# Two attention mixers and an output projection: the exponential's bias taken in VectorE's pass over the scores, one region for transposed weights, and an output projection in one-bank halves

## The chip, the cores and the metric

One Trainium2 chip; the kernel runs on one of its cores. The metric is the device time in microseconds of one execution. The program is compiled once, in one launch, and all its work is on the chip.

## What is computed

One layer of an encoder is applied to two request groups with the same weights: the prompt (2048 rows of 1024) and the sample (512 rows of 1024). Cut to what matters:

```python
h = rmsnorm(x, g_pre) * (1 + scale) + shift          # scale, shift, gate from silu(c) @ w_ada + b_ada
qa, ka, va, ga, qb, kb, vb, gb = split(h @ w_in)     # A: 8 heads of 64; B: 4 heads of 2 x 64
# A: three dilated windows (128, 1), (512, 4), (2048, 16), mixed by their softmax denominators
ya = dilated_mixture(rope(qa), rope(ka), va) * silu(ga)
# B: dense, two softmax maps per head
p = softmax(q @ k.T / 8)
a = p[map 0] - lam * p[map 1]
yb = rmsnorm(a @ vb, g_sub) * (1 - lam_init) * silu(gb)
y = concat(ya, yb) @ w_out
x = x + gate * rmsnorm(y, g_post)
```

## The kernel before

The work is cut into eight units, taken in the order A, B, A, B, ... (`ORDER`). A unit is two heads of A or one head of B, for both request groups. Each unit runs over five superblocks of 512 rows: four of the prompt (`p`), one of the sample (`s`). An item of B is 128 rows of queries against all keys (four items a superblock); an item of A is 128 rows of one head against its windows (eight items a superblock). Numbers are held as a high and a low half of 16 bits, so a product is made of two or three matrix products.

`ItemB.front` (lines 558 to 613) makes, for each of two maps, scores in tiles of 1024 columns (`sc`, PSUM, three tiles of two banks; two tiles a map for the prompt). L584 takes the maximum of each tile on VectorE, L587 on GpSimd makes the bias of the exponential from the maxima of both tiles, L592 on ScalarE takes the exponential with that bias into an `pp` buffer (five of 4 KB) and adds up the denominators. L609 combines the two maps, L611 writes the high half (`hi`), which a DMA transposes into a tile `at`; `tail1` (L619) does the same for the low half. `tail2` (L623 to L645) multiplies the transposed weights with V: 48 matmuls at L631, then a Square and a Copy on ScalarE and three small steps on GpSimd. `tail3` scales, transposes on TensorE (L652), multiplies by the gate into `yt`, and after the fourth item `y_out` writes `y` to DRAM.

`ItemA.front` has its scores at L686 and L692; L698 and L700 on VectorE add the masks in float32 and take the maxima in one pass each, L704 on GpSimd makes the bias, L707 on ScalarE the exponential. `tail1` (L710) normalises into a high and a low half and transposes both by DMA (L725, L726); `tail2` multiplies with V after every fourth item (L742, L748).

`run_items` sets the order of an item's steps beside those of the items before it: the item's first scores; at "mid" `tail2` and `tail3` of the item two before if that is an A item, or `tail3` alone if it is a B item, then `tail1` of the item just before; the second scores; at "late" `tail2` of the item just before if that is a B item. The pool `at` has three buffers of the largest tile, 6 KB; each item of B and each head of A takes two tiles.

Beside the items, as "fill", run the projections of the next superblock (`qg_proj`) and of the next unit (`kv_proj`), in PSUM tiles `pj` of one bank, of which there is one. `interleave` emits items and fill in proportion to their costs (`mc`, `fc`). In the last unit there is no next unit, and from the third superblock on the fill is the output projection (`out_proj`) of the superblock two before, in tiles of 128 rows: `y_first` loads `y` into a `w` buffer (four of 8 KB, which also hold the projection's weights and the rows `GG`) and splits it (L872, L873); 48 matmuls at L889 fill a score tile; Square (L896), the norm's factor (L898 to L901), a product (L902) and a sum (L903) follow, and L904 stores. Eight tiles remain for the end (L1052). The program is scheduled by the framework from this order of emission; each engine and SP's DMA queue run their instructions in order.

## Time and profile before

| | us |
|---|---|
| median of 3 runs | 2272.92 |
| lowest and highest run | 2272.75, 2280.08 |
| the profiled execution, its own time | 2281.88 |
| its span, first to last instruction | 2280.1 |
| TensorE busy | 1896.0 (83%) |
| VectorE busy | 1491.4 (65%) |
| ScalarE busy | 1191.5 (52%) |
| GpSimd busy | 533.1 (23%) |
| mean granted clock of TensorE | 0.933 |

PE is TensorE's matmuls, PEld its weight loads, DVE is VectorE, ACT ScalarE, POOL GpSimd, SP the queue that issues DMAs. A wait "X <- Y" is idle time of X's engine that ended when Y's work was done. Durations come from the one profiled execution, and sums are made against its time.

### The profile page before, as it was taken

What the parts mean: (1) busy time and instruction counts of PE and PEld (TensorE: products, weight loads), DVE (VectorE), ACT (ScalarE), POOL (GpSimd) and SP (SyncE); (2) the same over time, 40 slices, a digit from 0 to 9 for tenths busy, and PEclk for the clock granted to TensorE, in tenths of its full rate; (3) what the DMA queues carried; (4) which work ended last, traced back from release to release, by engine and by line L of the source; (5) the groups of instructions that cost most, each with busy time, mean ns of one, the idle gap of its engine ahead of it and who ended that gap; (6) DMA issues with size and microseconds to landing.
All of it is one profiled execution on the core that took longest, in us unless ns stands there. A gap on an engine that the chain in (4) does not pass through costs nothing. (4 is left out here: it accounts for less than half of the span.)

```text
span 2280.1 us, 47414 instructions
## 1 busy us (share of the span) xinstructions
PE 1896.0 (83%) x18545; PEld 1291.5 (57%) x18545; DVE 1491.4 (65%) x3084; ACT 1191.5 (52%) x2238; POOL 533.1 (23%) x1369
## 2 busy tenths in 40 slices
PE   4878888888889888887888798887887887678988
PEld 2665665555666665565676655555666554334433
DVE  3775566788856558777664578876565578555533
ACT  3555554566655546665654466664555466434321
POOL 1222122223322222222421122323222132111200
PEclk8989999999999999998999899999999998789989
DMA  8488895666779877666778766688898586354433
GB/s 325 167 278 165 163 211 118 129 132 137 161 141 187 148 196 139 134 139 149 143 166 162 172 145 148 119 184 200 180 181 191 123 161 134 70 142 101 139 118 119
DMA packets 726833, 360.11 MB, mean 158 GB/s; under 512 B 639808, under 2 KB 686672, under 8 KB 723152
## 3 DMA queue, kind: packets, MB, share of 16 engines
q1 hardware_dynamic: 726608, 357.08, 68.4%
q8 instruction: 145, 2.38, 0.4%
q14 instruction: 80, 0.66, 0.1%
HBM read 164.79 MB, written 36.97 MB: 88 GB/s over the span
## 5 line engine op out<-in xcount | busy, mean ns | idle before, releaser
L439 PE MATMUL pj<-w,h 128*128 128x256 f16 x3840 | 480.9, 283 | 33.0 <-DVE sg L539 11.4
L439 PEld LDWEIGHTS <-h 128*128 128x128 f16 x3840 | 382.0, 102 | 110.4 <-issue 46.9
L584 DVE TENSOR_REDUCE mx<-sc 128x1 f32<-128x1024 f32 (+1 forms) x288 | 329.9, 1159 | 119.9 <-PE sc L582 119.3
L592 ACT ACTIVATE pp<-sc,nb,us 128x1024 f32<-128x1024 f32 (+1 forms) x288 | 330.4, 1150 | 135.0 <-POOL nb L587 133.4
L631 PE MATMUL pv<-V,at 128*128 128x128 f16 x3072 | 223.7, 232 | 70.6 <-DMA at<-hl 60.9
L631 PEld LDWEIGHTS <-at 128*128 128x128 f16 x3264 | 209.7, 104 | 118.4 <-DMA at<-hl 84.0
L513 PE MATMUL pj<-w,h 128*128 128x128 f16 x3840 | 246.1, 222 | 14.6 <-ACT q L519 6.6
L724 DVE SCALAR_TENSOR_TENSOR hl<-pp,Z,hl 128x640 f16<-128x640 f32 (+2 forms) x160 | 141.6, 887 | 173.9 <-DMA at<-hl 125.1
L534 PE MATMUL pj<-h,w 128*128 128x512 f16 x960 | 230.8, 395 | 22.8 <-ACT q L519 22.8
L513 PEld LDWEIGHTS <-h 128*128 128x128 f16 x3840 | 227.1, 100 | 37.9 <-issue 33.6
L722 ACT ACTIVATE hl<-pp,Z 128x640 f16<-128x640 f32 (+2 forms) x160 | 130.9, 824 | 185.7 <-DMA at<-hl 151.6
L576 PE MATMUL sc<-K,Qc 128*128 128x512 f16 x512 | 160.3, 393 | 65.2 <-ACT pp L592 64.8
L422 POOL TENSOR_TENSOR rp<-q,tab_sb 128x64 f32<-128x64 f32 x160 | 68.9, 431 | 598.3 <-ACT q L445 408.1
L611 ACT ACTIVATE hl<-pp,rz 128x1024 f16<-128x1024 f32 (+1 forms) x144 | 156.1, 1096 | 67.6 <-issue 50.9
L619 DVE SCALAR_TENSOR_TENSOR hl<-pp,rz,hl 128x1024 f16<-128x1024 f32 (+1 forms) x144 | 174.3, 1222 | 22.0 <-ACT hl L611 12.4
L707 ACT ACTIVATE pp<-pp,nb,us 128x640 f32<-128x640 f32 (+2 forms) x160 | 146.2, 914 | 74.3 <-POOL nb L704 73.3
L534 PEld LDWEIGHTS <-w 128*128 128x128 f16 x960 | 94.5, 101 | 140.3 <-issue 48.2
L609 DVE SCALAR_TENSOR_TENSOR pp<-pp,rz,pp 128x1024 f32<-128x1024 f32 (+1 forms) x144 | 170.9, 1224 | 1.8
L889 PEld LDWEIGHTS <-w 128*128 128x128 f16 x960 | 94.5, 99 | 118.0 <-issue 8.9
L587 POOL TENSOR_SCALAR nb<-mx,us 128x1 f32<-128x1 f32 x160 | 87.4, 547 | 266.1 <-DVE mx L584 245.9
L704 POOL TENSOR_SCALAR nb<-mx,us 128x1 f32<-128x1 f32 x160 | 74.3, 465 | 211.6 <-DVE mx L700 169.8
L889 PE MATMUL sc<-raw,w 128*128 128x512 f16 x480 | 112.9, 392 | 4.0 <-ACT pp L592 3.2
(198 smaller groups left out, 2752.6 us busy)
## 6 DMA issues: line engine op xcount, KB each, us to landing
h<-hp SPq DMA_DIRECT2D x124, 512.0 KB, 5.6
pp<-in_x_p_dram SPq DMA_DIRECT2D x32, 512.0 KB, 5.3
raw<-in_w_in_dram SPq DMA_DIRECT2D x8, 2048.0 KB, 8.6
h<-hs SPq DMA_DIRECT2D x32, 512.0 KB, 5.7
out_dram<-pp SPq DMA_DIRECT2D x20, 512.0 KB, 2.8
at<-hl SPq DMA_TRANSPOSE x608, 3.2
hp<-h SPq DMA_DIRECT2D x4, 2048.0 KB, 8.0
yp<-yt SPq DMA_DIRECT2D x32, 256.0 KB, 2.4
```

The lines of the kernel that those rows point to most:

```text
L439: mm(ps[:, jj, :], lhsT=hT[:, a, k, j * P:(j + 1) * P], rhs=w[:, k, b, :], start=(k == 0 and i == 0), stop=(k == KT - 1 and i == 2))
L513: mm(ps[:, jj, 0:128], lhsT=hT[:, a, k, j * P:(j + 1) * P], rhs=w[:, k, b, 0:128], start=(k == 0 and i == 0), stop=(k == KT - 1 and i == 2))
L534: mm(ps, lhsT=w[:, k, b, 128:256], rhs=hT[:, a, k, :], start=(k == 0 and i == 0), stop=(k == KT - 1 and i == 2))
L576: mm(ps[:, n * 512:(n + 1) * 512], lhsT=Qc[:, j, m, 0, :], rhs=K[:, t:t + 4, m, :], start=True, stop=False)
L584: V.reduce_max(mx[:, hf:hf + 1], ps[:, :HW], axis=AX.X)
L592: act(pt[m, hf][:, :HW], pss[hf][:, :HW], AF.Exp, scale=u["sc"], bias=nb, accum_out=Z[:, 2 * m + hf:2 * m + hf + 1])
L609: V.scalar_tensor_tensor(a, a, rz[:, 2:3], pt[0, hf][:, :HW], op0=ALU.mult, op1=ALU.add)
L611: act(hi[:, :HW], a, AF.Copy, scale=rz[:, 3:4])
L619: V.scalar_tensor_tensor(lo[:, :HW], a, sg, hi, op0=ALU.mult, op1=ALU.subtract)
L631: mm(po[:, :128], lhsT=a[:, k, :], rhs=Vv[:, k, 128 * b:128 * b + 128], start=(k == 0 and i == 0), stop=(k == NT - 1 and i == 2))
L707: act(sb[:, :NA], sb[:, :NA], AF.Exp, scale=u["sc"], bias=nb, accum_out=Z[:, 0:1])
L889: mm(ps[:, 512 * h:512 * h + 512], lhsT=a[:, k, :], rhs=b, start=(k == 0 and i == 0), stop=(k == KT - 1 and i == 2))
```

## The change

In B the pass over a score tile becomes one VectorE instruction that multiplies the scores by the negated scale, writes them back over the tile in PSUM and keeps the minimum; the pass over the second tile starts from the first's minimum, which is then the bias. In A both masked passes multiply by the negated scale and take the minimum, the second from the first's; the query's scale and the masks are adapted, and the masks are stored in 16 bits. The GpSimd instruction is gone in both, and the exponential takes scale -1. The pool `at` becomes one region of 24 KB, cut in three pairs of 4 KB tiles for B and two pairs of 6 KB tiles for A. B's V products (`tail2`) go from "late" of the next item to "mid" of the item after that, `tail3` from "mid" to "late" there. The output projection is one generator over all tiles: it starts in the second superblock of the last unit as far as `y` has been made (`y_made`), gets a budget per superblock (`OPC`), works in halves of one bank in `pj`, and takes `w` buffers for `x` and the result while items run. After the items PSUM is divided anew, with five `pj` banks.

```diff
@@ -26,9 +26,10 @@
 MCA = [1, 1]
-PPB, HLB, ATB, WPB, HB = 5, 4, 3, 4, 2
+PPB, HLB, WPB, HB = 5, 4, 4, 2
 AQ = 1
 LEAD = [0, 0, 0, 0]
+OPC = [0, 20, 24, 24, 30]
 ORDER = (0, 4, 1, 5, 2, 6, 3, 7)
@@ -45,6 +46,7 @@
     SMAX = max(SQ.values())
+    NU = len(ORDER)
     NTM = SMAX // P
@@ -54,11 +56,28 @@
     hl = ctx.enter_context(tc.tile_pool(name="hl", bufs=HLB))
-    at = ctx.enter_context(tc.tile_pool(name="at", bufs=ATB))
+    at = ctx.enter_context(tc.tile_pool(name="at", bufs=1))
     tn = ctx.enter_context(tc.tile_pool(name="tn", bufs=6))
...
     dr = ctx.enter_context(tc.tile_pool(name="dr", bufs=1, space=DRAM))
+    at_buf = at.tile([P, 12288], F16, tag="at", name="at")
+    at_n = {3: 0, 2: 0}
+    def at_pair(n, *dims):
+        i = at_n[n]
+        at_n[n] = (i + 1) % n
+        w = 12288 // n // 2
+        out = []
+        for x in range(2):
+            t = at_buf[:, (2 * i + x) * w:(2 * i + x) * w + math.prod(dims)]
+            names = "abc"[:len(dims)]
+            out.append(t.rearrange(f"p ({' '.join(names)}) -> p {' '.join(names)}",
+                                   **dict(zip(names[1:], dims[1:]))))
+        return out
     PS = {}
@@ -320,12 +339,14 @@
             V.reciprocal(rs, s[:, 2:3])
+            smul(s[:, 1:2], s[:, 1:2], 2.0 * LN2)
             m0, m9 = (0, 992) if r == "p" else (480 - 32 * (SQ[r] // P - 1), 480 + SQ[r] // 4)
-            mk = T(qp, [P, m9 - m0 + 768], F32, "mask" + r, bufs=1)
-            nc.sync.dma_start(mk[:, 0:m9 - m0], m23[:, m0:m9])
-            nc.sync.dma_start(mk[:, m9 - m0:], m1.rearrange("p a b -> p (a b)"))
-            V.tensor_scalar(mk, mk, rs, LN2, op0=ALU.mult, op1=ALU.mult)
+            mk = T(qp, [P, m9 - m0 + 768], BF16, "mask" + r, bufs=1)
+            for src, dst in ((m23[:, m0:m9], mk[:, 0:m9 - m0]), (m1.rearrange("p a b -> p (a b)"), mk[:, m9 - m0:])):
+                t = T(pp, [P, 1024], F32, "pp")[:, 0:src.shape[1]]
+                nc.sync.dma_start(t, src)
+                V.tensor_scalar(dst, t, rs, 0.5, op0=ALU.mult, op1=ALU.mult)
             u["m23"], u["m0"] = mk[:, 0:m9 - m0], m0
@@ -516,7 +537,9 @@
             q32 = T(ev, [P, 2, 2, 64], F32, "q32")
-            act(q32.rearrange("p a b d -> p a (b d)"), ps[:, :, 0:128], AF.Copy, scale=2.0 ** -19)
+            act(q32.rearrange("p a b d -> p a (b d)"), ps[:, :, 0:128], AF.Copy,
+                scale=2.0 ** -19 * (1.0 if g >= 4 else 0.5 / LN2))
             rope(q32, TAB0[r] + t0)
@@ -542,10 +565,13 @@
     yam = C([P, sum(NSB.values()), 8], F32, "yam")
+    y_made = {}
     def y_out(r, g, c, y):
...
         nc.sync.dma_start(y_dram[r][c][:, g, :], y)
+        y_made[r, c] = y_made.get((r, c), 0) + 1
@@ -566,7 +592,7 @@
             for m in range(2):
-                mx = T(tn, [P, 2], F32, "mx")
+                nb = T(tn, [P, 2], F32, "nb")
                 pss = []
@@ -581,15 +607,15 @@
                            start=False, stop=True)
-                    V.reduce_max(mx[:, hf:hf + 1], ps[:, :HW], axis=AX.X)
+                    V.tensor_scalar(ps[:, :HW], ps[:, :HW], u["nsc"], nb[:, 0:1] if hf else 3e38,
+                                    op0=ALU.mult, op1=ALU.min, accum_out=nb[:, hf:hf + 1])
                     yield 0.43 * (HW // 512)
-                nb = T(tn, [P, 1], F32, "nb")
-                nc.gpsimd.tensor_scalar(nb, mx[:, 0:1], mx[:, NH - 1:NH], u["nsc"], op0=ALU.max, op1=ALU.mult)
                 if m == 0:
...
                     pt[m, hf] = T(pp, [P, 1024], F32, "pp")
-                    act(pt[m, hf][:, :HW], pss[hf][:, :HW], AF.Exp, scale=u["sc"], bias=nb,
+                    act(pt[m, hf][:, :HW], pss[hf][:, :HW], AF.Exp, scale=-1.0, bias=nb[:, NH - 1:NH],
                         accum_out=Z[:, 2 * m + hf:2 * m + hf + 1])
@@ -601,8 +627,7 @@
             nc.gpsimd.tensor_tensor(rz[:, 3:4], rz[:, 0:1], sigc, op=ALU.mult)
-            self.ah = T(at, [P, S // P, P], F16, "at")
-            self.al = T(at, [P, S // P, P], F16, "at")
+            self.ah, self.al = at_pair(3, S // P, P)
             self.lo = []
@@ -693,18 +718,17 @@
             sb = self.sb = T(pp, [P, 1024], F32, "pp")
-            mx = T(tn, [P, 2], F32, "mx")
+            nb = T(tn, [P, 2], F32, "nb")
             mo = 480 - 32 * b + P * k0 - u["m0"]
             V.tensor_tensor_reduce(sb[:, :Cc], ps[:, o:o + Cc], u["m23"][:, mo:mo + Cc],
-                                   1.0, -3e38, ALU.add, ALU.max, mx[:, 0:1])
+                                   u["nsc"], 3e38, ALU.add, ALU.min, nb[:, 0:1])
             V.tensor_tensor_reduce(sb[:, Cc:NA], ps[:, m1],
                                    u["m1"][:, 0 if b == 0 else 2 if b == NB - 1 else 1, :],
-                                   1.0, -3e38, ALU.add, ALU.max, mx[:, 1:2])
-            nb = T(tn, [P, 1], F32, "nb")
-            nc.gpsimd.tensor_scalar(nb, mx[:, 0:1], mx[:, 1:2], u["nsc"], op0=ALU.max, op1=ALU.mult)
+                                   u["nsc"], nb[:, 0:1], ALU.add, ALU.min, nb[:, 1:2])
             yield "mid"
             self.Z = Z = T(tn, [P, 4], F32, "Z")
-            act(sb[:, :NA], sb[:, :NA], AF.Exp, scale=u["sc"], bias=nb, accum_out=Z[:, 0:1])
+            act(sb[:, :NA], sb[:, :NA], AF.Exp, scale=-1.0, bias=nb[:, 1:2], accum_out=Z[:, 0:1])
             yield "late"
@@ -713,8 +737,7 @@
             if ("ah", h) not in st:
-                st["ah", h] = T(at, [P, 4, Cc // P + 2, P], F16, "at")
-                st["al", h] = T(at, [P, 4, Cc // P + 2, P], F16, "at")
+                st["ah", h], st["al", h] = at_pair(2, 4, Cc // P + 2, P)
             smul(Z[:, 1:2], Z[:, 0:1], 2.0 ** -14)
@@ -780,16 +803,15 @@
                 if x == "mid":
+                    if p2:
+                        yield from p2.tail2()
                     if isinstance(p2, ItemA):
-                        yield from p2.tail2()
-                        yield from p2.tail3()
-                    elif p2:
                         yield from p2.tail3()
...
                 elif x == "late":
-                    if isinstance(p1, ItemB):
-                        yield from p1.tail2()
+                    if isinstance(p2, ItemB):
+                        yield from p2.tail3()
                 else:
@@ -874,33 +896,44 @@
     def out_proj(tiles):
-        nxt = y_first(*tiles[0])
-        yield 0.0
+        nxt = None
         for n, (r, c, j) in enumerate(tiles):
+            while nxt is None:
+                if y_made[r, c] == NU:
+                    nxt = y_first(r, c, j)
+                else:
+                    yield 0.65
             yh, yl = nxt
+            nxt = None
             s = YS[r, c]
-            xt = T(pp, [P, D], F32, "pp")
+            if PS["w"] == 512:
+                xt, jk = T(pp, [P, D], F32, "pp"), T(pp, [P, D], F32, "pp")
+            else:
+                t = T(wp, [P, 2, D], F32, "w")
+                xt, jk = t[:, 0, :], t[:, 1, :]
             nc.sync.dma_start(xt, xv[r][c, :, j, :])
-            ps = PT([P, PS["w"]], "sc")
+            ss = T(tn, [P, 2], F32, "ss2")
             for h in range(2):
+                ps = PT([P, 512], "pj")
                 for k in range(KT):
...
                     for i, (a, b) in enumerate(((yh, wh), (yh, wl), (yl, wh))):
-                        mm(ps[:, 512 * h:512 * h + 512], lhsT=a[:, k, :], rhs=b,
+                        mm(ps, lhsT=a[:, k, :], rhs=b,
                            start=(k == 0 and i == 0), stop=(k == KT - 1 and i == 2))
                     yield 0.65
-                    if h == 0 and k == 0 and n + 1 < len(tiles):
+                    if nxt is None and n + 1 < len(tiles) and y_made[tiles[n + 1][:2]] == NU:
                         nxt = y_first(*tiles[n + 1])
-            jk = T(pp, [P, D], F32, "pp")
-            ss = T(tn, [P, 1], F32, "ss")
-            act(jk, ps, AF.Square, accum_out=ss)
+                sq = T(hl, [P, 512], F32, "hl")
+                act(sq, ps, AF.Square, accum_out=ss[:, h:h + 1])
+                V.tensor_mul(jk[:, 512 * h:512 * h + 512], ps, GG[r][:, 512 * h:512 * h + 512])
             v = T(tn, [P, 1], F32, "rv")
-            V.tensor_scalar(v, ss, s[:, 2:3], EPS, op0=ALU.mult, op1=ALU.add)
+            V.tensor_add(v, ss[:, 0:1], ss[:, 1:2])
+            V.tensor_scalar(v, v, s[:, 2:3], EPS, op0=ALU.mult, op1=ALU.add)
             o = T(tn, [P, 1], F32, "ro")
...
             nc.gpsimd.tensor_tensor(o, o, s[:, 0:1], op=ALU.mult)
-            V.scalar_tensor_tensor(jk, ps, o, GG[r], op0=ALU.mult, op1=ALU.mult)
-            V.tensor_add(jk, jk, xt)
+            V.scalar_tensor_tensor(jk, jk, o, xt, op0=ALU.mult, op1=ALU.add)
             nc.sync.dma_start(ov[r][c, :, j, :], jk)
@@ -951,7 +984,16 @@
     NS = len(SBS)
-    NU = len(ORDER)
+    outp = out_proj([(r, c, j) for r, c in SBS for j in range(4)])
+    def upto(gen, cost):
+        while cost > 0:
+            x = next(gen, None)
+            if x is None:
+                return
+            cost -= x
+            yield x
     g0 = ORDER[0]
@@ -1020,6 +1062,8 @@
                 side = chain(load_wo(1), call(load_gg))
+            if i == 0:
+                at_n[3] = 0
             if i == 0 and g2 is not None:
@@ -1039,17 +1083,20 @@
                         fl.append(call(load_v1, r2, g2, c2))
-            if g2 is None and i >= 2:
-                tiles = [(*SBS[i - 2], j) for j in range(4)]
-                fl.append(out_proj(tiles))
-                fc += 11 * len(tiles)
+            if g2 is None and i >= 1:
+                fl.append(upto(outp, OPC[i]))
+                fc += OPC[i]
             main = run_items(items(r, g, c) + ([None, None] if n + 1 == NU and i + 1 == NS else []))
...
             interleave(main, mc, weave(chain(*fl), side), fc, LEAD[2 * (r == "p") + (g < 4)])
-    run(out_proj([(*SBS[k], j) for k in (-2, -1) for j in range(4)]))
+    for x in outp:
+        if x == 0.1:
+            break
+    psum(512, 1, 5, 2)
+    run(outp)
 # ---- launch: one core; inputs and outputs as the reference has them ----
```

## Rows read from the trace of the kernel before

**Rows 1.** The page's first part: busy time, share of the span and instructions of each engine.

```profile
PE 1896.0 (83%) x18545; PEld 1291.5 (57%) x18545; DVE 1491.4 (65%) x3084; ACT 1191.5 (52%) x2238; POOL 533.1 (23%) x1369
```

**Rows 2.** Busy time by stretches: start and end in us, length, then busy us and instructions of PE, PEld, DVE, ACT and POOL, the granted clock, the DMA engines' share and GB/s. The stretches begin with a superblock's first exponential: units A, B, A, B, A, B, A, then the last unit's five superblocks and, from 2181.00, what remains after the last item.

```profile
169.70:374.30 204.60, 172.32 (x2066) 128.25 (x2058) 121.21 (x381) 103.18 (x193) 42.26 (x125) 0.96 0.80 171
374.30:641.60 267.30, 227.62 (x2177) 155.49 (x2175) 207.68 (x302) 163.17 (x315) 80.96 (x194) 0.95 0.64 136
641.60:845.30 203.70, 174.18 (x2120) 134.36 (x2121) 120.51 (x384) 105.01 (x201) 45.51 (x130) 0.94 0.84 171
845.30:1109.10 263.80, 225.13 (x2192) 151.85 (x2190) 208.90 (x310) 163.59 (x312) 79.04 (x191) 0.95 0.65 139
1109.10:1319.50 210.40, 178.23 (x2128) 136.34 (x2126) 122.69 (x385) 106.45 (x205) 43.95 (x133) 0.93 0.78 164
1319.50:1589.30 269.80, 230.69 (x2259) 156.48 (x2260) 211.41 (x310) 164.95 (x317) 79.38 (x197) 0.97 0.71 155
1589.30:1804.60 215.30, 179.58 (x2140) 132.65 (x2133) 125.66 (x391) 111.08 (x213) 48.50 (x128) 0.94 0.84 179
1804.60:1864.00 59.40, 50.28 (x521) 32.58 (x519) 45.21 (x58) 35.59 (x63) 19.10 (x41) 0.97 0.76 163
1864.00:1914.30 50.30, 42.18 (x404) 24.94 (x404) 42.53 (x55) 35.62 (x64) 13.33 (x37) 1.00 0.67 128
1914.30:2021.10 106.80, 78.39 (x454) 40.30 (x454) 58.69 (x77) 40.89 (x70) 14.36 (x32) 0.81 0.47 111
2021.10:2119.00 97.90, 76.38 (x451) 40.40 (x449) 56.77 (x72) 40.72 (x68) 14.61 (x31) 0.84 0.42 106
2119.00:2181.00 62.00, 53.56 (x310) 26.80 (x310) 31.91 (x55) 22.08 (x52) 14.08 (x36) 0.95 0.45 135
2181.00:2280.10 99.10, 87.74 (x389) 39.17 (x389) 35.69 (x50) 17.88 (x24) 5.90 (x16) 0.93 0.33 117
```

**Rows 3.** The table of waits over the whole execution: engine, what it was about to write and the line, what ended the wait, us in total, times, longest.

```profile
ACT pp L592 <- POOL nb L587: 133.4, 86, 7.7
...
ACT pp L707 <- POOL nb L704: 73.3, 65, 5.3
PE sc L576 <- ACT pp L592: 69.9, 69, 10.1
...
PE pv L631 <- DMA at<-hl: 67.2, 38, 9.8
...
PE pv L742 <- DMA at<-hl: 44.6, 31, 3.9
```

**Rows 4.** The same table for TensorE in the last unit alone, from 1804.6 us to the end.

```profile
PE pv L631 <- DMA at<-hl: 33.1, 13, 9.8
...
PE sc L576 <- ACT pp L592: 11.1, 11, 2.4
```

**Rows 5.** Groups of instructions by line and shape: line, engine, operation, out<-in, shapes, count, busy us, mean ns of one, idle us of the engine before them and what ended it.

```profile
L584 DVE TENSOR_REDUCE mx<-sc 128x1 f32<-128x1024 f32 x256 | 308.6, 1218 | 109.0 <-PE sc L582 108.6
...
L587 POOL TENSOR_SCALAR nb<-mx,us 128x1 f32<-128x1 f32 x160 | 87.4, 547 | 266.1 <-DVE mx L584 245.9 <-DVE ag L855 8.0 <-DVE rz L601 4.9
...
L902 DVE SCALAR_TENSOR_TENSOR pp<-sc,ro,w 128x1024 f32<-128x1024 f32 x20 | 25.6, 1282 | 11.6 <-POOL ro L901 11.3
...
L873 DVE SCALAR_TENSOR_TENSOR w<-w,ys 128x1024 f16<-128x1024 f32 x20 | 25.0, 1281 | 7.7 <-ACT w L872 7.7
...
L698 DVE DVE_READ_ACCUMULATOR2_ANT mx<- 128x1 f32 x160 | 13.0, 81 | 0.0
```

**Rows 6.** VectorE's timeline around 679 us: start, duration, engine, line, operation; the second instruction reads what the first writes.

```profile
679.11 0.15 DVE L99 TENSOR_SCALAR Z<-Z 128x1 f32<-128x1 f32 x1 [0.15 <-ACT pp L707]
679.30 0.16 DVE L720 RECIPROCAL Z<-Z 128x1 f32<-128x1 f32 x1
```

**Rows 7.** The timeline from 680.9 us, in an A unit: two DMA transposes that SP issues, and between them the end of a head's V products on TensorE.

```profile
680.94 1.21 SPq L725 DMA_TRANSPOSE at<-hl  x1
...
684.29 1.06 PE L748 MATMUL pv<-at,V 128*128 128x128 f16 x16
...
685.32 1.25 SPq L726 DMA_TRANSPOSE at<-hl  x1
```

**Rows 8.** The DMA issues by line: out<-in, count, KB each, median us from issue to landing.

```profile
w<-yp SPq DMA_DIRECT2D x16, 512.0 KB, 4.3
...
maskp<-in_m_dram SPq DMA_DIRECT2D x4, 496.0 KB, 6.7
```

**Rows 9.** TensorE's timeline from 1926 us, in the last unit's third superblock; in brackets the idle time before and what ended it.

```profile
1930.47 1.04 PE L631 MATMUL pv<-V,at 128*128 128x128 f16 x8 [3.92 <-DMA at<-hl]
...
1945.43 1.04 PE L631 MATMUL pv<-V,at 128*128 128x128 f16 x8 [3.82 <-DVE ys L99]
...
1949.69 1.06 PE L889 MATMUL sc<-raw,w 128*128 128x512 f16 x2
```

**Rows 10.** SP's own waits in the last unit, from 1804 us: what it was about to issue, what ended the wait, us in total, times, longest.

```profile
SPq L871 <- PE sc L889: 76.1, 12, 15.4
```

**Rows 11.** ScalarE's timeline in the tail: the Square that follows a tile's last matmul, the split of a later tile's `y`, and the next tile's Square.

```profile
2240.41 1.02 ACT L896 ACTIVATE pp<-sc 128x1024 f32<-128x1024 f32 x1 [4.91 <-PE sc L889]
...
2244.74 1.15 ACT L872 ACTIVATE w<-w,ys 128x1024 f16<-128x1024 f32 x1 [3.21 <-DMA w<-ys]
...
2250.77 1.02 ACT L896 ACTIVATE pp<-sc 128x1024 f32<-128x1024 f32 x1 [4.88 <-PE sc L889]
```

## The prediction

> **What bounds the kernel now.** I read the busy shares first: TensorE is busy 83% of the span, VectorE 65%, ScalarE 52% [rows 1]. No engine is full, so the question is what TensorE, the fullest, waits for. The table by stretches comes next [rows 2]: A and B units alternate in its first seven rows, the last six are the last unit, superblock by superblock, with the tail. TensorE idles 130 us in the 834 us of the A units (834.0 - 704.3 busy), 117 us in the 801 us of the B units (800.9 - 683.4) and 87 us in the 475.5 us of the last unit (475.5 - 388.5). The last unit is the worst place: its third and fourth stretches take 107 and 98 us at a granted clock of 0.81 and 0.84, where the second takes 50 us at 1.00. The table of waits says what ended TensorE's idle time [rows 3]: scores wait 69.9 us for an Exp to free a score tile, B's V products 67.2 us for transposed weights, A's V products 44.6 us. Of the first two, 11.1 and 33.1 us lie in the last unit [rows 4], so 58.8 and 34.1 us are the B units'. ScalarE's Exp in turn waits 133.4 and 73.3 us for GpSimd's bias [rows 3]. So this is a loop of latencies (scores, maximum, bias, Exp, score tile free again), with TensorE its fullest member and VectorE (628.0 of 800.9 us in the B units [rows 2]) the second.
>
> **The bias.** Removed: 160 bias instructions of 547 ns on GpSimd in B [rows 5] and as many in A, and with each two hand-overs between engines ahead of Exp. Added: in B the maximum (1,218 ns on 1,024 scores) becomes a pass that also writes the negated scaled scores over the score tile. The trace of before shows no VectorE instruction that writes PSUM. Bounds for one pass: from below 1,218 ns, the reduction that reads the same tile; from above 2.50 us, the reduction and a separate pass of 1,282 ns as L902 makes from PSUM [rows 5]. It is one instruction with one stream in and one out, so L902's 1,282 is the nearest row; with the accumulator read of 81 ns [rows 5], most of which overlaps its neighbour, I take 1.34 us: +0.12 us. The Trainium skill ("VectorE: DVE Perf Modes", The TRN2 errata) gives 120 cycles plus one per element for an op out of PSUM, by estimate 1.19 us here; by that the pass would cost no more than the reduction, and nothing would be added; the page has no figure for a PSUM destination.
>
> The three B units make 192 passes of 1,024 and 24 of 512: 192 x 0.12 + 24 x 0.07 = +25 us on VectorE, then 653 us busy. A second pass now reads the first's minimum. Such a reader starts 0.04 us after its writer's end [rows 6]; with the accumulator read that is some +0.15 us, 160 times in A, 24 us on a VectorE that idles 344 of 834 us there [rows 2]: hidden. Behind it on VectorE wait the splits of the weights, whose transposes are wanted an item later. If that cover were gone (VectorE full), the price is 25 + 24 us. In exchange Exp starts earlier by the bias, 0.55 us and up (GpSimd runs it in turn behind rotary and power steps), so score tiles come free sooner: half of the 58.8 us, 29 us, goes; bounds 0 and 58.8. What is late next there is VectorE's own queue: I put 10 us back.
>
> **One region, and V products an item later.** Before, three 6 KB buffers serve tiles that come in pairs, so the second tile of a pair waits for the products of the item or head just before. In A one sees it: a `hi` transpose is issued at 680.94, the next `lo` only at 685.32, when the other head's V products end (684.29 + 1.06) [rows 7]; SP's queue is in order, so what lies behind waits too. With two pairs in A and three in B no transpose waits for the item just finished. In B the 48 V products of an item move from behind the next item's second scores to between the first and second scores of the item after that. Their Square and Copy on ScalarE and three GpSimd steps move with them; the output's transpose and the `y` store on SP move behind the second scores. That is half an item later, some 6 us of a 55 us stretch with four items, against waits of 1.4 us on average (34.1 us in 38 - 13 waits [rows 3, 4]): I let 27 of the 34.1 us go, bounds 0 and 34. TensorE also gets work at the very point where it waits for a score tile; that is part of the 29 above. In A the products keep their place, and the last transpose is still one short item ahead, so I let half of the 44.6 us go: 22 us, bounds 0 and 45. Shorter holes should return a little clock: 3 in B, 3 in A. **B: -29 + 10 - 27 - 3 = -49; A: -25.** Bounds: B 0 and -95, A +10 (dependent passes) and -55. The masks now pass through the exponentials' five buffers; a load of 6.7 us [rows 8] may hold two of them at the start and in three later units. I take +3 us, bounds 0 and +10.
>
> **Output projection.** Before, a tile holds one of three score tiles and two of five exponential buffers through its 48 matmuls and its evacuation, and each group of four tiles starts only when its stretch comes. The trace shows it: from 1,926 to 1,950 us TensorE does items alone, with holes of 3.9 and 3.8 us, and the first output matmuls start at 1,949.69 [rows 9]. In this unit SP stands 76.1 us before loads of `y` that wait for a tile's matmuls, with the transposes queued behind them [rows 10]. After, tiles use the projection's bank in halves, other buffers, and begin one stretch earlier. Work per tile is equal: 48 matmuls, 10.36 us at full clock (2,240.41 to 2,250.77 [rows 11]); the evacuation runs in halves, a few tenths of a microsecond more, beside TensorE's work.
>
> I build the unit anew from its second stretch (TensorE 42.2 us at clock 1.00: one query projection and four items) plus tiles. The budgets 20, 24, 24 and 30, at 10.5 a tile, give 1.5, 2.3, 2.3 and 2.9 tiles; the first is less by 4.6, since the query projection ends at 11 of 31 of the stretch and the first superblock's last output comes at half. That leaves 11 tiles for the tail where 8 were. First stretch 59.4 - 2.4 = 57; second 42.2 + 15.6 + 5 idle = 63; third and fourth 42.2 + 23.8 + 5 = 71 each; the short one 12 (53.6 less four tiles of 10.4) + 30 + 6 = 48; tail 11 x 10.36 + 10 for its start and last store = 124. Sum 434 against 475.5: **-42**. Bounds: -65, if its idle time falls to the tail's share; 0, if the following holds. Until the last query projection one weight tile and the gate rows keep two of the four `w` buffers; a tile's `y` and its `x` take the other two, so the next `y` is loaded only after a tile's matmuls: 4.3 us of load [rows 8] and 1.15 + 1.28 of splitting [rows 5, 11], some 7 us, about 6 times, with SP waiting and the transposes behind it. I take it as covered by the items, 42 us of TensorE work a stretch. Uncovered it is 42 us and eats the gain.
>
> **Sum.** -49 - 25 - 42 + 3 = -113 us against the profiled execution (2,281.88 us; span 2,280.1): 2,169. The median of the runs is 2,272.92, lower by 0.4%; in its terms 2,169 x 0.9961 = 2,160.
>
> **Rivals.** (1) *The body gives nothing*: the longer VectorE passes, now chained, eat what the bias gave, and transposes still come late because SP and the DMA engines (0.64 to 0.84 busy in the body [rows 2]) set their pace. For: VectorE is the second fullest. Against: it idles 173 us in the B units. Left are the last unit's 42 and some 10 of A: 2,224; with a last unit that gives little, within 0.5% of before. (2) *The last unit gives nothing* (the `w` buffers and SP's queue, above): 2,160 + 42 = 2,202. (3) *Slower*: the pass in place is dear. VectorE's busiest stretch is 42.5 of 50.3 us, 85% [rows 2]; grant it 90%, and B breaks even when 628 + 192 d = 721, at d = 0.48, a pass of 1.70 us. From there each 0.1 us costs 21 us in B and some 6 in the last unit, so the other gains (64) are used up at a pass of 1.94 us; at the upper bound of 2.50 us it is 2,273 + 5.6 x 27 = 2,424. For: no row shows such a write. Against: L902 and the reduction both run near 1.2 ns an element, whatever they write. (4) *The clock follows*. In A and B the granted clock is 0.93 to 0.97 [rows 2]; with two levels, 2 x (1 - clock) of each stretch ran at 1.2 GHz, about 165 us in all, half of it lost. If fewer holes give half of that back, 40 us more go: 2,120. The rule behind it is the Trainium skill's ("TensorE: Matmul & The Clock Gate", What's actually happening): the slow clock is the default and activity releases it. The rows agree as far as they go: 0.81 in the stretch with the holes of 3.9 and 3.8 us, 1.00 in the one before.
>
> **How the numbers follow.** Forecast 0.48 (2,130 to 2,200); body nothing 0.20; last unit nothing 0.10; slower 0.10; clock 0.12. A measurement of this kernel tells 0.5% (11 us) from no change. Faster: 0.48 + 0.10 + 0.12 and 0.13 of the first rival, 0.83; same 0.07, the rest of it; slower 0.10. The range of 8 in 10 runs from 2,088, inside the clock's case, to 2,262, where the first rival turns into no change; outside lie the dear pass, that rest, and the case that the clock and all lower bounds come together.
>
> **What would show it.** Bias: the pass near 1.34 us; ScalarE's wait before Exp, 133.4 us, under 60. V products: TensorE's waits for transposed weights in the B units under 15 us, in A about 22. Last unit: its third stretch near 71 us at a clock over 0.95, eleven tiles after the last items. The prediction is wrong if the pass is over 1.7 us, if SP still stands before loads of `y` with TensorE idle behind it, or if the scores' wait for Exp stays at 59 us in B.

## The result and the profile after

| | before | after |
|---|---|---|
| median, us (runs beside each other) | 2273.43 | 2194.36 (2190.65 to 2201.74) |
| ratio, 95% interval | | 0.965 [0.9619, 0.9681] |
| span of the profiled execution, us | 2280.1 | 2192.6 |
| up to the first item | 169.7 | 177.5 |
| four A units | 833.8 | 813.6 |
| three B units | 801.1 | 719.2 |
| last unit with the tail | 475.5 | 482.2 |

The kernel is 3.5% faster where 2,160 us (5.0%) were forecast. The total hides the main thing: the B units gave 82 us where 49 were forecast, and the last unit, from which 42 were to come, lost 7. Against the terms of the prediction's sum, B came out 33 us better; A came out 5 us worse, the start 5 and the last unit 49. That the time lies as near the forecast as it does is luck in part, since the two largest errors have opposite signs.

Busy time by stretches of after, with the columns of [rows 2]: the three B units, then the last unit's first to fourth superblock, what follows up to the last `y_out` (2,072.8), and the tail.

```profile
378.40:620.80 242.40, 221.01 (x2240) 154.11 (x2238) 214.82 (x385) 156.81 (x313) 62.13 (x155) 0.97 0.77 160
...
816.80:1054.70 237.90, 217.42 (x2224) 151.90 (x2221) 214.10 (x383) 156.80 (x313) 60.76 (x154) 0.99 0.78 168
...
1253.90:1492.80 238.90, 219.10 (x2221) 151.22 (x2222) 211.51 (x376) 156.90 (x313) 59.35 (x156) 0.99 0.79 166
...
1710.30:1765.10 54.80, 44.18 (x403) 26.67 (x402) 43.51 (x70) 33.30 (x61) 11.66 (x27) 0.94 0.75 167
1765.10:1812.60 47.50, 30.99 (x230) 16.36 (x230) 41.29 (x72) 28.84 (x53) 9.35 (x16) 0.80 0.56 115
1812.60:1902.40 89.80, 69.03 (x479) 36.94 (x477) 59.54 (x91) 39.58 (x74) 12.12 (x28) 0.88 0.43 97
1902.40:1988.90 86.50, 67.33 (x503) 37.19 (x501) 51.34 (x85) 38.66 (x74) 9.25 (x28) 0.86 0.44 95
1988.90:2072.80 83.90, 70.17 (x412) 35.07 (x409) 38.41 (x78) 26.90 (x70) 13.56 (x32) 1.00 0.46 123
2072.80:2192.60 119.80, 107.69 (x486) 48.26 (x486) 46.19 (x80) 24.74 (x52) 8.16 (x22) 0.96 0.42 134
```

Read the B units first, against [rows 2]. Their length less TensorE's busy time is its idle time: 719.2 - 657.5 = 62 us, where it was 117. Busy time itself fell too, from 683.4 to 657.5 us with nearly the same matmuls, while the granted clock rose from 0.95 to 0.97 up to 0.97 to 0.99. So 82 = 56 of holes + 26 of busy time. The clock explains some 16 of these 26: by the trace's clock records TensorE was busy for 55 us of the B units at the lower of its two levels before, for 23 us after, and a matmul takes twice as long there (0.43 us against 0.22, in the timeline below). The other 10 stay open. In the last unit the clock fell in the first two stretches, from 0.97 to 0.94 and from 1.00 to 0.80, and rose in all that follow, as from 0.81 and 0.84 to 0.88 and 0.86 in the next two; weighted by length the whole unit went from 0.90 to 0.92.

The table of waits of after, whole execution (it answers to [rows 3]).

```profile
ACT pp L618 <- DVE sc L611: 82.1, 65, 4.8
...
PE sc L602 <- ACT pp L618: 42.3, 48, 5.3
...
PE pv L765 <- DMA at<-hl: 24.5, 16, 3.8
...
PE pv L656 <- DMA at<-hl: 18.8, 17, 2.6
```

Exp (L618) now waits for VectorE's pass, 82 us instead of 133 for GpSimd. Scores wait 42.3 us instead of 69.9, B's V products 18.8 instead of 67.2, A's 24.5 instead of 44.6. The same table for TensorE in the last unit alone (it answers to [rows 4]):

```profile
PE sc L602 <- ACT pp L618: 26.8, 19, 5.3
...
PE pj L922 <- ACT w L894: 10.4, 3, 5.4
PE pj L922 <- DVE w L929: 8.2, 7, 1.9
PE pv L656 <- DMA at<-hl: 5.1, 4, 2.6
```

So of the scores' wait only 15.5 us is left in the B units (58.8 before), and the last unit has more than twice its old 11.1. Groups of instructions of after, with the columns of [rows 5]: Exp, the two forms of the new pass, A's second masked pass, the read of the new pass's accumulator.

```profile
L618 ACT ACTIVATE pp<-sc,nb 128x1024 f32<-128x1024 f32 x256 | 282.4, 1107 | 91.0 <-DVE sc L611 74.6 <-DVE p L168 8.2 <-DVE rz L627 5.1
...
L611 DVE TENSOR_SCALAR_CACHE_REDUCE sc<-sc,us,nb 128x1024 f32<-128x1024 f32 x128 | 172.5, 1348 | 23.8 <-PE sc L608 11.9 <-ACT pp L618 10.2 <-issue 0.7
...
L611 DVE TENSOR_SCALAR_CACHE_REDUCE sc<-sc,us 128x1024 f32<-128x1024 f32 x128 | 165.0, 1289 | 6.9 <-PE sc L608 5.7
...
L726 DVE CUSTOM_DVE_ANT_0 pp<-sc,maskp,nb 128x256 f32<-128x256 f32 x128 | 67.8, 538 | 0.5
...
L611 DVE DVE_READ_ACCUMULATOR sc<-sc,us 128x1 f32 x160 | 22.6, 141 | 0.1
```

The timeline of after between the last unit's first two output tiles (columns as in [rows 9]):

```profile
1829.36 0.38 PE L922 MATMUL pj<-K,w 128*128 128x512 f16 x1
1829.77 0.54 SPq L893 DMA_DIRECT2D w<-yp  x1
1829.78 0.60 ACT L928 ACTIVATE hl<-pj 128x512 f32<-128x512 f32 x1 [6.16 <-PE pj L922]
...
1830.50 0.69 DVE L929 TENSOR_TENSOR w<-pj,w 128x512 f32<-128x512 f32 x1 [4.83 <-ACT hl L928]
...
1833.96 1.15 ACT L894 ACTIVATE w<-w,ys 128x1024 f16<-128x1024 f32 x1 [3.49 <-DMA w<-yp]
...
1835.16 1.04 PE L922 MATMUL pj<-raw,w 128*128 128x512 f16 x2 [5.42 <-ACT w L894]
...
1836.48 7.35 PE L922 MATMUL pj<-raw,w 128*128 128x512 f16 x22
```

The first tile's last matmul starts at 1,829.36; only then is the next `y` loaded, split, and used: 5.4 us in which TensorE does nothing, and then 22 matmuls in 7.35 us (334 ns each, at a granted clock of 0.66: they start every 0.43 us up to 1,841.5, where the clock rises, and every 0.22 us from there; 24 take 5.34 us at 1.00, in e10 below).

### The profile page after: what moved, and what is told of

Its sections match the earlier page's. It is cut to its first block, busy times and chain, and to the rows that moved or that the text cites. A ratio compares the mean times of both kernels' runs of the same rounds, so it can differ in the third digit from the quotient of the medians.

```text
span 2192.6 us, 47675 instructions
## 1 busy us (share of the span) xinstructions
PE 1868.2 (85%) x18545; PEld 1275.3 (58%) x18545; DVE 1541.7 (70%) x3428; ACT 1156.7 (53%) x2278; POOL 387.2 (18%) x1049
## 5 line engine op out<-in xcount | busy, mean ns | idle before, releaser
L460 PE MATMUL pj<-w,h 128*128 128x256 f16 x3840 | 488.9, 284 | 43.2 <-DVE Vs L476 12.9
L618 ACT ACTIVATE pp<-sc,nb 128x1024 f32<-128x1024 f32 (+1 forms) x288 | 304.1, 1060 | 104.1 <-DVE sc L611 82.1
L534 PE MATMUL pj<-w,h 128*128 128x128 f16 x3840 | 244.9, 222 | 18.6 <-ACT q L541 9.2
L656 PEld LDWEIGHTS <-at 128*128 128x128 f16 x3264 | 202.7, 102 | 72.0 <-issue 42.7
L656 PE MATMUL pv<-V,at 128*128 128x128 f16 x3072 | 209.5, 227 | 37.4 <-DMA at<-hl 18.8
L557 PE MATMUL pj<-h,w 128*128 128x512 f16 x960 | 221.1, 384 | 16.3 <-ACT q L541 16.3
L611 DVE TENSOR_SCALAR_CACHE_REDUCE sc<-sc,us 128x1024 f32<-128x1024 f32 (+1 forms) x160 | 188.2, 1182 | 10.9 <-PE sc L608 9.7
L611 DVE TENSOR_SCALAR_CACHE_REDUCE sc<-sc,us,nb 128x1024 f32<-128x1024 f32 x128 | 172.5, 1348 | 23.8 <-PE sc L608 11.9
L731 ACT ACTIVATE pp<-pp,nb 128x640 f32<-128x640 f32 (+2 forms) x160 | 131.7, 823 | 76.9 <-DVE nb L726 75.4
L922 PE MATMUL pj<-raw,w 128*128 128x512 f16 x480 | 116.4, 400 | 17.8 <-ACT w L894 10.4
L711 PE MATMUL sc<-K,Qc 128*32 128x512 f16 (+1 forms) x1024 | 99.5, 364 | 19.5 <-DMA Qc<-tq 13.8
```

The costliest lines, as they stand in the source:

```text
L460: mm(ps[:, jj, :], lhsT=hT[:, a, k, j * P:(j + 1) * P], rhs=w[:, k, b, :], start=(k == 0 and i == 0), stop=(k == KT - 1 and i == 2))
L534: mm(ps[:, jj, 0:128], lhsT=hT[:, a, k, j * P:(j + 1) * P], rhs=w[:, k, b, 0:128], start=(k == 0 and i == 0), stop=(k == KT - 1 and i == 2))
L557: mm(ps, lhsT=w[:, k, b, 128:256], rhs=hT[:, a, k, :], start=(k == 0 and i == 0), stop=(k == KT - 1 and i == 2))
L611: V.tensor_scalar(ps[:, :HW], ps[:, :HW], u["nsc"], nb[:, 0:1] if hf else 3e38, op0=ALU.mult, op1=ALU.min, accum_out=nb[:, hf:hf + 1])
L618: act(pt[m, hf][:, :HW], pss[hf][:, :HW], AF.Exp, scale=-1.0, bias=nb[:, NH - 1:NH], accum_out=Z[:, 2 * m + hf:2 * m + hf + 1])
L656: mm(po[:, :128], lhsT=a[:, k, :], rhs=Vv[:, k, 128 * b:128 * b + 128], start=(k == 0 and i == 0), stop=(k == NT - 1 and i == 2))
```

## The experiments

Stage sums of each profiled execution in us (from the first exponentials of the units, as in the table above), and the ratio of the timed runs to before on the same chip:

| kernel | ratio [95%] | start | A | B | last unit |
|---|---|---|---|---|---|
| e1_bias_only | 0.9736 [0.969, 0.9782] | 178.0 | 831.5 | 739.5 | 463.0 |
| e2_region_only | 1.0028 [1.0006, 1.0049] | 178.6 | 824.6 | 820.4 | 455.6 |
| e3_outproj_only | 1.0109 [1.007, 1.0148] | 171.3 | 836.3 | 802.2 | 498.9 |
| e4_bias_region | 0.949 [0.9443, 0.9537] | 177.1 | 813.2 | 721.2 | 454.4 |
| e5_tiles_last | 0.9569 [0.953, 0.9608] | 179.0 | 817.0 | 720.6 | 469.7 |
| e6_exp_scale_tile | 0.9715 [0.9674, 0.9756] | 176.9 | 815.2 | 760.4 | 454.1 |
| e7_bias_by_gpsimd | 0.9809 [0.9773, 0.9846] | 178.5 | 810.3 | 792.1 | 460.2 |
| e8_own_buffers | 0.9631 [0.9594, 0.9668] | 177.8 | 819.1 | 719.6 | 482.6 |
| e9_schedule_only | 0.9625 [0.9601, 0.965] | 178.3 | 815.2 | 724.2 | 473.6 |
| e10_halves_only | 0.9594 [0.9556, 0.9631] | 179.4 | 812.5 | 721.5 | 469.1 |
| e11_v_not_later | 0.9723 [0.9696, 0.9751] | 176.8 | 812.4 | 764.2 | 461.2 |
| e12_masks_not_pp | 0.9478 [0.9454, 0.9502] | 176.6 | 816.8 | 719.3 | 449.7 |

**The three parts, each alone, and the first two together.** e1 has the lines for the bias, the query's scale and the masks; e2 the region and the later V products (with the masks in 16 bits); e3 the output projection; e4 is e1 and e2.

```diff
 e1: -V.reduce_max(mx[:, hf:hf + 1], ps[:, :HW], axis=AX.X)
     +V.tensor_scalar(ps[:, :HW], ps[:, :HW], u["nsc"], ..., accum_out=nb[:, hf:hf + 1])
 e2: +self.ah, self.al = at_pair(3, S // P, P)
     +if p2: yield from p2.tail2()      # at "mid", an item later
 e3: +ps = PT([P, 512], "pj")           # per half; one generator, OPC
```

> The kernel before with the bias part alone (VectorE's pass writes the negated scaled scores and keeps the minimum, GpSimd's step is gone, masks in 16 bits). Theory: the B units gained 82 us in the whole change, and the bias carries the larger half of it, since every Exp starts earlier and is 90 ns shorter: about 2,225 us, B units near 755 us in sum. Rival: the chain was held by late transposes, so the bias alone gives little: above 2,255 us, B units above 785 us, and TensorE's wait for transposed weights stays near 67 us.

> The kernel before with the 24 KB region and the V products an item later alone; to make room for the region it also takes the 16-bit masks with the query's scale, which change no step of the items. Theory: TensorE's wait for transposed weights falls from 67 to about 20 us, and the B units lose some 35 us: about 2,235 us. Rival (the bias carries nearly all of it): above 2,260 us, the waits for Exp growing by what the waits for transposes lose.

> The kernel before with the new output projection alone. Theory (the last unit gains nothing from it, because a tile's y is loaded only after the tile before has ended, and bursts of 24 matmuls hold up ScalarE and VectorE): the last unit stays at 475 to 485 us, total 2,268 to 2,285 us. Rival (it gains some 40 us, and the other two parts cost the last unit as much): about 2,235 us.

> The changed kernel with the output projection of before: bias and region together. Theory (the new output projection is worth nothing in its place): 2,180 to 2,200 us, the same as the changed kernel within 0.5%, and the last unit between 465 and 485 us. Rival (the new output projection gains 40 us that something else in the last unit eats): 2,230 us or more.

The bias alone gives 2.6%, 62 us of it in B and 13 in the last unit. Region and later V products alone give nothing: A -9, last unit -20, but B **+19**; its V products still wait 40.7 us for transposes, where 20 were expected. Together they give 5.1%, and there the second part is worth 18 us in B. The output projection costs 23 us in the last unit alone and 28 on top of e4. e4 is faster than the kernel with all three parts (0.949 against 0.965), which was not expected: they were to be the same. Why the second part hurts without the first shows in part in e2's table of waits for ScalarE, in its group of bias steps, and in its timeline in a B unit:

```profile
ACT pp L614 <- POOL nb L609: 170.9, 83, 6.1
...
L609 POOL TENSOR_SCALAR nb<-mx,us 128x1 f32<-128x1 f32 x160 | 118.3, 740 | 292.9 <-DVE mx L606 275.2 <-DVE zs L620 11.5 <-DVE rz L623 4.9
...
403.49 0.36 POOL L609 TENSOR_SCALAR nb<-mx,us 128x1 f32<-128x1 f32 x1 [7.14 <-DVE mx L606]
...
491.19 2.47 DVE L640 SCALAR_TENSOR_TENSOR hl<-pp,rz,hl 128x1024 f16<-128x1024 f32 x2
...
491.69 2.15 POOL L609 TENSOR_SCALAR nb<-mx,us 128x1 f32<-128x1 f32 x1
...
493.87 1.20 ACT L614 ACTIVATE pp<-sc,nb,us 128x1024 f32<-128x1024 f32 x1 [3.95 <-POOL nb L609]
```

Exp's wait for GpSimd's bias grew from 133.4 us [rows 3] to 170.9, in the B units alone from 73.8 to 128.4. The bias step itself grew from 547 ns [rows 5] to 740. The step at 403.49 is one of those that run alone; the step at 491.69 runs beside VectorE's passes with two inputs in SBUF (L640; L630 is another) and takes 2.15 us. In e2's B units the 38 of 120 steps that meet such a pass take 1.73 us on average, the other 82 0.39; in before 25 meet one (1.25 us). That lengthens the steps by 29 us. What stands ahead of the bias in GpSimd's queue did not grow: from the maximum to the bias step's start it is 57 us in sum over B, 73 in before. The rest of the longer wait stays open.

**What in the bias gives it.** e6 is e4 with Exp's factor -1 from a tile of one column; e7 is e4 with the bias handed once through GpSimd.

```diff
 e6: -act(pt[m, hf][:, :HW], pss[hf][:, :HW], AF.Exp, scale=-1.0, ...)
     +act(pt[m, hf][:, :HW], pss[hf][:, :HW], AF.Exp, scale=mone, ...)
 e7: +nc.gpsimd.tensor_scalar(nbg, nb[:, 0:1], nb[:, NH - 1:NH], 1.0, op0=ALU.min, op1=ALU.mult)
```

> The kernel with the bias and region parts alone (2,163 us), with one edit: the exponential's scale of -1 is read from a [128, 1] tile, as the scale was before, instead of being a constant in the instruction. Theory (the shorter Exp, 1,107 against 1,197 ns, comes from the constant and is worth something in the loop of score tiles): Exp back at 1.20 us in B and 1.02 us on 768 columns in A, and some 15 us more: about 2,178 us. Rival (the constant explains the 90 ns, but ScalarE has room): within 5 us of 2,163. If Exp stays at 1.11 us, it is not the constant.

> The kernel with the bias and region parts alone (2,163 us), with one edit: in the B items the finished bias is passed once through GpSimd (a minimum of the two entries, which changes no value) before the exponential reads it. Theory (what the bias part gave in B is the GpSimd step in the loop, together with the steps that stand before it in GpSimd's queue now that the V products' power steps fall there): about 60 us more in B, 2,220 us or over. Rival (it is Exp's length and the chained minimum): under 2,185 us.

e6 loses 39 us in B. Its Exp, with the tile as an operand (`mone`), takes 90 ns more than the 1,107 above:

```profile
L592 ACT ACTIVATE pp<-sc,nb,us 128x1024 f32<-128x1024 f32 x256 | 305.6, 1197 | 124.0 <-POOL nb L587 123.2 <-DVE pp L609 0.6
...
L615 ACT ACTIVATE pp<-sc,nb,mone 128x1024 f32<-128x1024 f32 x256 | 305.4, 1197 | 104.8 <-DVE sc L608 81.2 <-issue 10.1 <-DVE rz L624 5.2
```

The first line is before's, where `us` is the operand. On B's 216 Exps that is 19 us of ScalarE. The other 20 stay open: with the added operand the framework also puts the instructions of all engines in another order than in e4. e7 loses 71 us in B for an instruction of 0.5 us; its instructions, too, come in another order than e4's, so the 71 us are not shown to be the step's alone. Its timeline in a B unit shows one place where the step costs more than its length:

```profile
493.24 0.14 DVE L606 DVE_READ_ACCUMULATOR sc<-sc,us,nb 128x1 f32 x1
494.74 0.28 ACT L660 ACTIVATE ojk<-pv 128x128 bf16<-128x128 f32 x1 [1.63 <-PE pv L653]
...
495.20 0.64 POOL L663 TENSOR_SCALAR rv<-ss,us 128x1 f32<-128x1 f32 x1 [7.25 <-ACT ojk L660]
...
495.94 0.29 POOL L610 TENSOR_SCALAR nbg<-nb 128x1 f32<-128x1 f32 x1
496.25 1.11 ACT L615 ACTIVATE pp<-sc,nbg 128x1024 f32<-128x1024 f32 x1 [0.98 <-POOL nbg L610]
```

The minimum is ready at 493.4, but GpSimd stands in front of `rv`, a step of the V products' tail, until 495.20; the bias behind it in the queue comes at 495.94. Such places are few: the tail's steps stand ahead of B's 120 biases for some 13 us in sum in e7, 22 in e2 and 36 in before. So this queue is not why the later V products, with their region, cost 19 us in B without the bias part (e2) and give 18 with it (e4). That the two parts act on each other is measured; the cause is shown no further than e2's longer bias steps.

**Region or later place.** e11 is e4 with the V products where they were; three pairs stay.

```diff
-                    if p2:
-                        yield from p2.tail2()      # "mid"
+                    if isinstance(p1, ItemB):
+                        yield from p1.tail2()      # "late"
```

> Bias and region parts with the old output projection, but the V products where they were (of the item before, after this item's Exps) instead of an item later; three pairs of transposed weights stay. Theory 'later' (what the pair of edits adds to the bias is the V products' own wait for the transposes, gone only with the later place): the B units go back to 735 to 742 us as with the bias alone, and 'V product <- DMA' waits come back; ratio 0.965 to 0.972 (2200 to 2216 us). Theory 'buffers' (the third pair is what freed the transposes): the B units stay at 718 to 725 us, ratio 0.948 to 0.952. The A units stay near 813 us by both.

B is 764.2, 43 us above e4 and even 25 above e1, where 'later' expected no more than e1's: the later place carries the gain, and 'buffers' falls. TensorE's waits in e11, where e4 has 17.8 us:

```profile
PE pv L651 <- DMA at<-hl: 58.4, 37, 5.0
```

Why three pairs at the old place are worse than three single buffers was not followed.

**The output projection.** e5 is the changed kernel with all budgets 0, so all 20 tiles come after the items. e8 gives each tile one `w` buffer instead of two (x in other buffers, the result over the tile's own `y`). e9 and e10, on e4, split the part in two; e10 also takes the change's `w` buffer for x and the result and its new division of PSUM.

```diff
 e5:  -OPC = [0, 20, 24, 24, 30]
      +OPC = [0, 0, 0, 0, 0]
 e8:  -t = T(wp, [P, 2, D], F32, "w")
      +t = T(kv, [P, 5, 256], F16, "V1", bufs=2)...     # x, by halves; jk = y32
 e9:  +ps = PT([P, PS["w"]], "sc")     # changed order, tile as before
 e10: +ps = PT([P, 512], "pj")         # old order, tile in halves
```

> The changed kernel with all budgets of the output projection at zero: no tile beside the items, all 20 after the last item. Theory (tiles beside the items cost more than they save, because their loads, halves and evacuations stand in the same in-order queues as the items' steps): four item stretches of about 50 us, the short one 25, 20 tiles of 10.4 and 12 for start and end, last unit about 450 us instead of 482: total about 2,162 us. Rival (overlap with the items is worth having and only the number of tiles per stretch is wrong): the tail grows by 9 tiles, 94 us, and the items get back at most 60: 2,225 us or more.

> The changed kernel with one edit in the output projection while items run: x goes in halves into the two V1 buffers, which no B unit uses, and the result is written over the tile's own y, so a tile needs one w buffer instead of two and the next y can be loaded early. Theory A (the w buffers were it: a tile's y was loaded only after the tile before had ended): last unit about 450 us, total 2,160 us, and SP's wait before loads of y (67.5 us) under 20. Theory B (the queues of VectorE and ScalarE behind bursts of 24 matmuls are it): last unit stays above 470 us, total above 2,180 us.

> Both with the bias and region parts; the output projection has the changed order (one generator of 20 tiles, budgets 0, 20, 24, 24, 30, next y load only when the next tile may start, the rest at the end) but each tile is computed as before: a whole score tile of PSUM, two pp buffers, one Square, one product, one add, and no division of PSUM anew at the end. Theory 'halves' (a half may not begin in the only pj bank until ScalarE's Square and VectorE's product have read the half before, so that every tile waits twice): the last unit goes back to that of the old output projection, 452 to 458 us, ratio 0.949 to before (2163 us). Theory 'order' (the tiles pulled by budgets, fewer of them beside the items): the last unit stays at 478 to 486 us, ratio 0.962 to 0.966 (2192 us). If each holds half of it, near 468 us and 0.956.

> The counterpart: bias and region parts, the old order of the tiles (groups of four from the third stretch on, eight at the end), but each tile in one-bank halves of pj with x and the result in a w buffer, and PSUM divided anew (five pj banks) before the last eight. Theory 'halves': the last unit is 478 to 486 us, ratio near 0.963 (2192 us), and matmuls of the halves wait for ScalarE's Square and VectorE's product while items run. Theory 'order': 452 to 458 us and 0.949 (2163 us), or some us less, since the last eight tiles have five banks.

e8 gains nothing, but it is not a clean test of the `w` buffers. SP's waits in the last unit, the changed kernel's before loads of `y`, then e8's before loads of `y` and of `x`:

```profile
SPq L893 <- PE pj L922: 67.5, 10, 12.6
...
SPq L893 <- PE pj L930: 36.4, 7, 8.4
...
SPq L918 <- DVE w L949: 85.1, 6, 26.9
```

The wait before `y` fell to 36.4 us, not under the 20 expected, and in its place SP stands 85.1 us before loads of `x`. TensorE's wait for a `y` that is split late fell from 10.4 to 4.4 us, and its wait for VectorE's product of a half rose from 8.2 to 16.7. e9 and e10 lie 19 and 15 us above e4, 34 in sum where both together cost 28: each theory holds about half. e5, with nothing beside the items at all, is faster than the changed kernel, though its last unit misses the 450 us expected. Its two stretches, up to the last `y_out` and after:

```profile
1716.60:1961.50 244.90, 178.58 (x1529) 106.77 (x1527) 191.45 (x312) 141.66 (x280) 47.25 (x112) 0.84 0.59 115
1961.50:2186.00 224.50, 212.49 (x975) 95.63 (x975) 88.64 (x159) 49.23 (x100) 14.76 (x40) 0.98 0.42 133
```

The items alone take 244.9 us with TensorE busy for 178.6; no engine is full (VectorE, the fullest, is busy for 191.5), which leaves their loop of latencies as what bounds them, at a clock of 0.84. Each kernel's time from the unit's start to its last `y_out` beyond that, by the tiles done until then, gives the price of a tile beside the items:

| | tiles | us | price of one |
|---|---|---|---|
| e4 (old form) | 12 | 355.6 | 9.2 |
| e10 (halves) | 12 | 370.5 | 10.5 |
| e9 (order) | 11 | 364.9 | 10.9 |
| changed kernel | 10 | 362.5 | 11.8 |

In the tail a tile costs 10.4 ([rows 11]). So a tile beside items is hidden hardly in the old form and not at all in the new. For the halves, e10 shows the hole within one tile:

```profile
2000.41 5.34 PE L911 MATMUL pj<-raw,w 128*128 128x512 f16 x24
...
2007.31 0.38 PE L911 MATMUL pj<-K,w 128*128 128x512 f16 x1 [0.95 <-DVE w L918]
```

24 matmuls end at 2,005.75; the second half starts 1.56 us later, when VectorE's product has left the only bank. By TensorE's waits in e10's last unit that is 12.9 us, beside 14.0 for a `y` that is split late, so e10's 15 us are not the halves' alone:

```profile
PE pj L911 <- ACT w L889: 14.0, 5, 5.4
...
PE pj L911 <- DVE w L918: 12.9, 10, 2.5
```

For the order, e9's timeline after its second tile:

```profile
1868.27 1.03 PE L656 MATMUL pv<-V,at 128*128 128x128 f16 x8 [6.58 <-DMA at<-hl]
...
1884.34 1.01 PE L602 MATMUL sc<-K,Qc 128*128 128x512 f16 x2 [4.68 <-ACT pp L618]
...
1904.24 1.01 PE L917 MATMUL sc<-raw,w 128*128 128x512 f16 x2 [8.04 <-ACT pp L618]
```

Two tiles are done by 1,846.8; the third starts at 1,904.24, although its `y` was made at 1,794.2, and in between the items run alone with holes of 6.6, 4.7 and, before the tile itself, 8.0 us. Its V products wait 20.1 us for transposes in the last unit, those of e4 5.3.

**The start, and the fastest version.** e12 is e4 with the first unit's mask pieces in the region for transposed weights instead of `pp`.

```diff
+                if g == ORDER[0]:
+                    t = at_buf[:, o:o + 2 * w].bitcast(F32)
```

> Bias and region parts with the old output projection (the fastest so far, 2163 us, 0.949), and the first unit's four mask pieces loaded into parts of the region for transposed weights, which is not in use before the first item, instead of pp buffers; the later units' as before. Theory 'pp' (the mask pieces hold four of the five pp buffers in which the next rows of x should land, so that the norm of the second super-block starts later): the start goes from 177 back to 169 to 172 us, the rest stays, 2154 to 2159 us, ratio 0.944 to 0.947. Theory 'own work' (the start is longer through the conversion itself or the order it takes in VectorE's queue, not the buffers): the start stays at 176 to 179 us and the time at 2160 to 2167 us.

The start stays at 176.6, so 'pp' falls; what makes it some 7 us longer with the new masks (e3, without them, has 171.3) stays open. The ratio, 0.9478 [0.9454, 0.9502], cannot be told from e4's. These two are the fastest versions: the change without its output projection.

## Why the prediction was right or wrong

**The failed step is the output projection (-42).** It built each stretch as TensorE's busy time, 42.2 us of items, plus 10.4 a tile, plus 5 us idle: 63, 71 and 71 us for the second to fourth. Measured: 47.5 with no tile finished, 89.8 and 86.5. Its sum of 434 us is 217 for the items, 93 for nine tiles beside them and 124 for the tail. By e5's items and the price of a tile the measured 482 us are 245, 118 for ten tiles, and 120. So the items' own loop was 28 us too short in the sum, 20 of them in the short last stretch (37.5 us in e5, where 12 + 6 stood), and the tiles 24. Work beside the items was taken to fill their holes, at TensorE's time; it comes on top, at 9.2 us a tile in the old form and 11.8 in the new. With the old form e4's last unit is 454.4 us: the other two parts gave this unit 21 us, which the prediction put at nothing, and the output projection took 28. The second stretch was to hold 1.5 tiles; the first superblock's `y` was made at 1,782.7, and the first tile started at 1,813.0, after that stretch.

The rival with the same sign, *the last unit gives nothing* (2,202), came near the time, and its mechanism is there in part, as one of the prediction's own signs of being wrong says: SP still stands 67.5 us before loads of `y` (76.1 before), and TensorE idles 10.4 us for a `y` that is split late. That is a quarter of the 42 us it was priced at, and what it is worth stays open, since e8 moved SP's wait to `x`. What e9 and e10 show instead is the order (19) and the halves with their buffers (15).

**Bias: right, the size too small.** The pass was put at 1.34 us; it takes 1.289 and 1.348. The Trainium skill's 120 cycles and one per element ("VectorE: DVE Perf Modes", The TRN2 errata), an estimate of 1.19 us, is 0.10 to 0.16 below it. ScalarE's wait was to fall under 60 and is 82.1, now for VectorE; but the scores' wait in B fell by 43 us, where 29 were taken. Not priced at all was an operand: with a constant for its factor, Exp takes 1,107 ns where it took 1,197 in before (L592, above; e6 has the same). The Trainium skill has it: "ScalarE: Activation LUTs", What ACT_TABLE_LOAD costs, says that each operand of one column adds about 93 ns; the runs agree with 90. It was there to be read, and e6 puts it, with the order that comes with it, at 39 us in B.

**V products later, and one region: right in B's waits (34.1 to 13.7 us, forecast 7 left) and in A (-20.2, forecast -25; e1 to e4 -18).** Wrong was to add it to the bias as a separate term. Alone it costs 19 us in B, with the bias it gives 18. The prediction has no term for what the move does to the bias steps that stay where they are; e2 shows 29 us of it, in steps that now meet VectorE's passes, and the rest is open.

**Clock.** Some 16 of B's 82 us are matmuls at a higher clock; 3 were put down. So the rival *the clock follows* came true in part, in B. It was to give 40 us in A and B together; in A the busy time fell by 4 us in all, from 704 to 700. The Trainium skill's rule ("TensorE: Matmul & The Clock Gate", What's actually happening: the slow clock is the default, activity releases it) agrees with these rows: 0.80 where TensorE is busy 31.0 of 47.5 us, 0.99 in B units where it is busy 91 to 92%.

**Start:** +7.8 where +3 was taken, within the bounds, for a reason that e12 did not bear out. *The body gives nothing* and *slower* fell with the pass's 1.35 us and B's 82.

## What to carry to other kernels

Before work is put beside a loop, learn what the loop takes alone: one bound by its latencies doesn't take in more work for free, even with TensorE idle a quarter of the time. Savings in one loop don't add: the later V products and their region were worth -19 or +18 us in B, by whether the bias part was there, so measure a part on top of the others and not alone. And price every changed operand, not only every changed instruction.

## What the runs showed of the hardware

A one-column operand in place of a constant costs time on both engines. ScalarE's Exp: 1,107 against 1,197 ns (e4, e6). VectorE: the new pass takes 1,289 ns with one such operand and 1,348 with two. The masked pass over 512 columns went from 682 to 743 ns with the factor from a tile, that over 256 from 417 to 538 with factor and starting value from tiles, some 60 ns each; the operation also went from maximum to minimum there, and no run parts the two. Masks in 16 bits alone changed nothing (683 and 417 in e2). The lines of before, then after's for 512 columns:

```profile
L698 DVE CUSTOM_DVE_ANT_0 pp<-sc,maskp 128x512 f32<-128x512 f32 x64 | 43.7, 682 | 2.9 <-PE sc L692 2.4
...
L700 DVE CUSTOM_DVE_ANT_0 pp<-sc,maskp 128x256 f32<-128x256 f32 x128 | 53.4, 417 | 0.0
...
L724 DVE CUSTOM_DVE_ANT_0 pp<-sc,maskp,us 128x512 f32<-128x512 f32 x64 | 47.3, 743 | 6.6 <-PE sc L717 6.3
```

A step of one column on GpSimd takes several times as long beside a VectorE pass with two inputs in SBUF: the bias step 0.39 us alone and 1.73 beside one in e2's B units, 0.39 and 1.25 in before's.
